# Where the lower halves of split matmul operands lie in on-chip memory

## The chip, the cores and the metric

The kernel runs on one core of one Trainium2 chip. The metric is the device time of one execution in microseconds (us), from three runs; beside them stands one profiled execution, from which all rows below come. In the profile PE is the matmul engine (TensorE) and PEld its weight loads, DVE is VectorE, ACT is ScalarE, POOL is GpSimd and SP is SyncE, which issues the transfers.

## The reference

One block of a diffusion transformer over 256 latent tokens and 256 context tokens, width 2048, all in float32. Cut to what matters here:

```
h  = modulate(rms_norm(x, norm_attn_w), sh_a, sc_a)        # also for ctx
q, k, v, u = split_projection(h @ w_in)                    # 2048 -> 2560
attn = latent_window_attention(q, k, v, kc, vc, attn_sink)
pool = multiscale_pool(u, pool_w, pool_scale)
x  = x + g_a * (concatenate([attn, pool]) @ w_out)         # 2048 -> 2048
hm = modulate(rms_norm(x, norm_mlp_w), sh_m, sc_m)
x  = x + g_m * (square(relu(hm @ w_up)) @ w_down)          # 2048 -> 8192 -> 2048
return rms_norm(x, final_norm_w)
```

The modulation vectors (sh, sc, g) come from `silu(c) @ w_ada + b_ada`.

## The kernel before

Every large product is made from split operands. An fp32 tile is cast to a shorter format (the upper part, `hi`, by ACT), and what is left over is its lower part (`lo = raw - hi`, by DVE). A product A*B then takes three matmuls into one accumulator, A_hi*B_hi, A_hi*B_lo and A_lo*B_hi, which the helper `mm3` issues at L288, L289 and L290. Each matmul instruction is preceded by a weight load of its stationary operand (128 columns); the other operand, 256 or 512 columns, moves through.

The weights stream from HBM in 1 MB tiles `raw` (five buffers), and are split in halves into `hi` and `lo` (six buffers each, `WeightStream.split_to`, L87 to L103). The stages, in the order of time, with the name of the accumulator that the profile shows:

- input projection: `ps_qu` (256 columns, weights stationary, activations `hhi`/`hlo` moving), `ps_k` (512 columns, the same way), `ps_v` (256 columns, weights moving);
- attention: scores `ps_s` (512 columns, keys `khi`/`klo` moving, queries `qs` stationary), transposes and `ps_o`;
- output projection: `ps_w` (512 columns, weights moving, the mixed activations `mx` stationary);
- the MLP. The first three of 16 column groups of w_up go through `mm3` at 256 columns. For the 13 others (`up_group`, L894) the upper and lower part of an activation tile `mx` lie side by side and move as one operand of 512 columns against `hi`, and then the upper part alone, 256 columns, against `lo`: for each quarter of the depth 16 matmuls of the first kind, then 16 of the second. `down_group` multiplies the activations `ahi`/`alo` (stationary) with w_down (`hi`/`lo` moving, 512 columns) through `mm3` into `ps_d`: eight groups b, each of 4 column blocks x 2 row halves x 8 depth tiles x 3 = 192 matmuls, 1536 in all, in which L288, L289 and L290 follow each other.

While one matmul runs, the weight load of the next one is already under way. The order on each engine is decided when the program is built. Tiles come from pools that are laid out in the order in which their tags are first asked for; `gap(pool, n)` asks for an unused tile of n bytes per partition, so that whatever follows lies n bytes further on. It computes nothing.

Of the kernel before, what the change touches and what calls it, by code (L numbers as in the profile page):

```python
# [9 lines left out]
F32R = mybir.dt.float32r  # L10
# [5 lines left out]
P = 128  # L16
D = 2048
KC = 16
T = 256
# [30 lines left out]
def gap(pool, n, name="gap"):  # L50

    pool.tile([P, n // 4], F32, tag=name, name=name, bufs=1)


class WeightStream:
# [27 lines left out]
    def split_to(self, n):  # L87
        nc = self.nc
        while self.n_half < min(n, len(self.halves)):
            i, h = self.halves[self.n_half]  # L90
            if i >= self.n_load:
                break
            raw = self.raw[i][:, 2 * h : 2 * h + 2, :]
            hi = self.pool.tile([P, 2, 512], F32R, tag="hi", name="hi", bufs=N_HALF)
            if not self.n_half:
                gap(self.pool, 320)
            lo = self.pool.tile([P, 2, 512], F32R, tag="lo", name="lo", bufs=N_HALF)
            nc.scalar.copy(hi, raw)  # L98
            nc.vector.tensor_tensor(lo, raw, hi.bitcast(F32), ALU.subtract)  # L99
            self.split[i, h] = (hi, lo)  # L100
            self.n_half += 1
# [23 lines left out]
def kernel(  # L125
# [223 lines left out]
    hpa = hpa_es.enter_context(tc.tile_pool(name="hpa", bufs=1, side="right", reuse_waits="tile"))  # L349
# [48 lines left out]
    def normalize(i):  # L398

        ss4 = stp.tile([P, 4], F32, tag="ss4", name="ss4", bufs=2)  # L400
        ss = stp.tile([P, 1], F32, tag="ss", name="ss", bufs=2)
        for q in range(4):
            junk = stp.tile([P, 512], F32, tag="junk", name="junk", bufs=2)
            xq = xh[i][:, 512 * q : 512 * q + 512]
            if q % 2:
                nc.scalar.activation(junk, xq, AF.Square, accum_out=ss4[:, q : q + 1])
            else:
                nc.vector.scalar_tensor_tensor(junk, xq, 1.0, xq, ALU.mult, ALU.mult, accum_out=ss4[:, q : q + 1])
        nc.vector.tensor_reduce(ss, ss4, axis=AX.X, op=ALU.add)
        r = rstd(stp, ss, 1)  # L410
        nc.vector.tensor_scalar(xh[i], xh[i], r, None, ALU.mult)
        for g in range(4):
            tp = bank("tp")
            for j in range(4):
                k = 4 * g + j
                nc.tensor.transpose(tp[:, P * j : P * j + P], xh[i][:, P * k : P * k + P], ident)
            nc.scalar.copy(xT[g][:, :, P * i : P * i + P], tp.rearrange("p (j t) -> p j t", j=4))
# [22 lines left out]
    def modulated(c_, streams=(0, 1)):  # L440

        pool = hpb if c_ in (2, 3, 6, 7) else hpa
        if 0 in streams:
            hhi = pool.tile([P, 2, 512], F32R, tag="hhi", name="hhi", bufs=2)
            if c_ in (0, 2):
                gap(pool, 320, "gaph")
            hlo = pool.tile([P, 2, 512], F32R, tag="hlo", name="hlo", bufs=2)
            hparts[c_] = hhi, hlo
        hhi, hlo = hparts[c_]
        for j in range(2):  # L450
            k = 2 * c_ + j
            xk = xT[k // 4][:, k % 4, :]
            for s in streams:
                v = xk[:, T * s : T * s + T]
                nc.vector.tensor_scalar(v, v, am_a[:, k, s : s + 1], sm_a[:, k, s : s + 1], ALU.mult, ALU.add)
            ts_ = slice(T * streams[0], T * streams[-1] + T)
            nc.scalar.copy(hhi[:, j, ts_], xk[:, ts_])  # L457
            nc.vector.tensor_tensor(hlo[:, j, ts_], xk[:, ts_], hhi[:, j, ts_].bitcast(F32), ALU.subtract)  # L458
            hs[k] = lambda s, j=j: (hhi[:, j, s], hlo[:, j, s])
# [72 lines left out]
    def run_in(op):  # L532
        if op[0] == "ada":
            c_, kg = op[1:]
            if kg == 0:
                adas[c_] = ada_attn(c_)
            adas[c_][kg]()
        elif op[0] == "mod":
            adas[op[1]][4]()
            modulated(op[1])  # L540
        elif op[0] == "kv":
            project_kv(*op[1:])
        elif op[0] == "qu":
            project_qu(*op[1:])
        elif op[0] == "mean":
            pool_mean(op[1])
        elif op[0] == "mixb":
            open_mixb()
        elif op[0] == "pool":
            in_w["pool"] = S.next("w")  # L550
        elif op[0] == "poolp":
            pool_project(op[1])
        elif op[0] == "pools":
            pool_split(op[1])
        else:
            run_late(1)

    mixa = hpb = None
    modulated(0, (0,))
    for op in in_ops:  # L560
        if op[0] == "ctx":
            normalize(2)
            normalize(3)
            modulated(0, (1,))
            xn_es.close()
            mixa = ctx.enter_context(tc.tile_pool(name="mixa", bufs=1, side="left", reuse_waits="tile"))
            gap(mixa, 192)
            hpb = hpb_es.enter_context(tc.tile_pool(name="hpb", bufs=1, side="left", reuse_waits="tile"))
            gap(hpb, 192)
        else:  # L570
            run_in(op)
    gap(hpa, 320)
    st_es.close()
    hpa_es.close()

# [222 lines left out]
    mp = ctx.enter_context(tc.tile_pool(name="mp", bufs=1, side="right", reuse_waits="tile"))  # L798
# [63 lines left out]

    def activation(pss):
        ahi = mp.tile([P, 4, T], F32R, tag="ahi", name="ahi", bufs=3)
        gap(mp, 64)
        alo = mp.tile([P, 4, T], F32R, tag="alo", name="alo", bufs=3)
        for m in range(4):
            t = mp.tile([P, T], F32, tag="act", name="act", bufs=2)
            if pss[m].shape[1] == T:
                nc.scalar.activation(t, pss[m], AF.Relu)  # L870
                nc.vector.tensor_tensor(t, t, t, ALU.mult)
            else:
                nc.scalar.copy(t, pss[m][:, T : 2 * T])
                nc.vector.tensor_tensor(t, pss[m][:, 0:T], t, ALU.add)
                nc.vector.scalar_tensor_tensor(t, t, 0.0, t, ALU.max, ALU.mult)
            nc.scalar.copy(ahi[:, m, :], t)
            nc.vector.tensor_tensor(alo[:, m, :], t, ahi[:, m, :].bitcast(F32), ALU.subtract)
        return ahi, alo

    def up_group():  # L880

        pss = [bank("ps_up") for _ in range(4)]
        for kg in range(4):
            w = S.next("w")
            for part in range(2):
                for m in range(4):
                    for j in range(4):  # L890
                        k = 4 * kg + j
                        wk = w(j, slice(P * m, P * m + P))[part]
                        ps, h = (pss[m][:, 0:T], hm[k][0]) if part else (pss[m], hm[k][2])
                        nc.tensor.matmul(ps, wk, h, start=part == k == 0, stop=part == 1 and k == KC - 1, skip_group_check=True)  # L894
        return activation(pss)

    def first_up_groups():

        banks = [bank("ps_up") for _ in range(6)]
        sums = [[banks[2 * f + m // 2][:, T * (m % 2) : T * (m % 2) + T] for m in range(4)] for f in range(3)]
        acts = []
        modulate_m(0)
        for kg in range(4):
            for f in range(3):
                w = S.next("w")
                if kg == f == 0:
                    with tc.issue_after(rb_ready.ins):  # L910
                        run_late(LATE_NORM)
                for m in range(4):
                    for j in range(4):
                        k = 4 * kg + j
                        mm3(sums[f][m], w(j, slice(P * m, P * m + P)), hm[k], k == 0 and m % 2 == 0, k == KC - 1)
                with tc.issue_after(rb_ready.ins):
                    run_late(LATE_UP[3 * kg + f])
                    if kg == 2 and f == 1:
                        run_late(1)
                if kg < 3 and f == 1:  # L920
                    modulate_m(kg + 1)
                if kg == 3:
                    acts.append(activation(sums[f]))
        return acts
# [133 lines left out]
```

## Time and profile before

| | us |
|---|---|
| three runs | 1160.4, 1165.46, 1166.04 |
| median of the three | 1165.46 |
| profiled execution, its own time | 1161.86 |
| span of the profiled execution | 1160.1 |
| PE busy | 1115.3 (96%) |
| DVE busy | 803.4 (69%) |
| ACT busy | 503.6 (43%) |

A matmul's time on the page (394 ns for 512 columns, say) goes from its start to its modelled end, and the next one starts long before that end. What a stream of matmuls costs is the distance from start to start, which the timeline gives; the page's mean cannot be multiplied by the count. A longer duration at the same number of columns does, however, go with a later start of the next matmul.

### The profile page before, as it was taken

The page shows a single profiled execution, that of the slowest core. Times are in us where ns is not written, and L with a number is a line of the kernel's source. Part 1 is how long each engine was busy: PE and PEld are TensorE (multiplying, and loading weights), DVE is VectorE, ACT ScalarE, POOL GpSimd, SP SyncE. Part 2 cuts the span into 40 slices and gives each one's busy share as a digit, 9 for nine tenths or more (in the row PEclk, how much of TensorE's full clock was granted, in tenths as well). Part 3 has the DMA queues.
Part 4 walks back from the last instruction along what each step waited for, and adds up shares of the span by engine and source line. Part 5 has one row for each costly group of instructions (what it writes and reads, how often), then busy time and mean ns, then how long its engine had stood idle before and what let it go on. Part 6 is the DMA issues. An engine that isn't in the chain of part 4 may idle for free.

```text
span 1160.1 us, 16052 instructions
## 1 busy us (share of the span) xinstructions
PE 1115.3 (96%) x6308; PEld 904.8 (78%) x6308; DVE 803.4 (69%) x1298; ACT 503.6 (43%) x760; POOL 40.4 (3%) x55
## 2 busy tenths in 40 slices
PE   3999999989999989999999999999999999999995
PEld 2767778845678869988888888888888888888884
DVE  5545567989786988886764884785664664587576
ACT  4532333357734433365443433443444443443452
POOL 1000001620000000000000000000000000000001
PEclk9899999989999989899999999999999999999998
DMA  9999897667898999968775775676566555655531
GB/s 337 317 328 340 298 311 258 218 232 271 278 378 276 312 316 358 353 225 267 267 268 190 252 257 188 235 251 231 182 189 199 192 181 184 199 191 189 183 107 73
DMA packets 174012, 286.64 MB, mean 247 GB/s; under 512 B 5609, under 2 KB 72353, under 8 KB 172785
## 3 DMA queue, kind: packets, MB, share of 16 engines
q1 hardware_dynamic: 172800, 279.55, 71.8%
q0 software_dynamic: 848, 5.55, 1.2%
q8 instruction: 49, 0.80, 0.3%
q10 hardware_dynamic: 288, 0.52, 0.1%
q14 instruction: 27, 0.21, 0.0%
HBM read 283.50 MB, written 2.10 MB: 246 GB/s over the span
## 4 chain that ended last, share of the span: by engine, by line
PE 81%; DVE 9%; DMA 6%; ACT 2%; issue 1%; SPq 1%; DVEq 0%; ACTq 0%
PE ps_up L894 25%; PE ps_d L288 10%; PE ps_d L289 10%; PE ps_d L290 10%; PE ps_ada L305 5%; DMA raw<-in_w_mlp_up_dram 3%; DVE lo L99 3%; PE ps_qu L288 2%; PE ps_qu L289 2%; PE ps_qu L290 2%; PE ps_o L738 2%; DMA raw<-in_w_in_dram 2%; DVE ada_v L327 1%; PE tp_p L727 1%; PE ps_w L288 1%
## 5 line engine op out<-in xcount | busy, mean ns | idle before, releaser
L99 DVE TENSOR_TENSOR lo<-raw,hi 128x1024 fp32r<-128x1024 f32 x330 | 396.8, 1224 | 223.1 <-ACT hi L98 216.1
L98 ACT CAST hi<-raw 128x1024 fp32r<-128x1024 f32 x330 | 337.5, 1051 | 407.3 <-PE ps_up L894 150.3
L288 PE MATMUL ps_d<-hi,ahi 128*128 128x512 f32 x512 | 201.6, 395 | 0.0
L289 PE MATMUL ps_d<-lo,ahi 128*128 128x512 f32 x512 | 201.0, 394 | 0.0
L894 PE MATMUL ps_up<-mx,hi 128*128 128x512 f32 x832 | 200.0, 392 | 0.0
L290 PE MATMUL ps_d<-hi,alo 128*128 128x512 f32 x512 | 198.4, 392 | 0.0
L894 PEld LDWEIGHTS ps_up<-mx,hi 128*128 128x128 f32 x832 | 153.4, 188 | 31.8 <-issue 1.9
L290 PEld LDWEIGHTS ps_d<-hi,alo 128*128 128x128 f32 x512 | 96.2, 188 | 22.8
L327 DVE SCALAR_TENSOR_TENSOR ada_v<-raw,c_sil,ada_v 128x512 f32<-128x512 f32 x135 | 100.8, 747 | 18.3 <-DMA raw<-in_w_ada_dram 16.8
L288 PEld LDWEIGHTS ps_d<-hi,ahi 128*128 128x128 f32 x512 | 96.2, 188 | 22.0
L289 PEld LDWEIGHTS ps_d<-lo,ahi 128*128 128x128 f32 x512 | 96.1, 188 | 21.2
L894 PEld LDWEIGHTS ps_up<-mx,lo 128*128 128x128 f32 x832 | 105.3, 189 | 4.0
L894 PE MATMUL ps_up<-mx,lo 128*128 128x256 f32 x832 | 106.6, 281 | 0.0
L288 PE MATMUL ps_qu<-hhi,hi 128*128 128x256 f32 x256 | 75.7, 296 | 5.4 <-ACT hhi L457 5.4
L305 PE MATMUL ps_ada<-raw,c_sil 128*32 128x512 f32 x480 | 73.1, 626 | 0.7 <-DMA raw<-in_w_ada_dram 0.7
L289 PE MATMUL ps_qu<-hlo,hi 128*128 128x256 f32 x256 | 72.9, 285 | 0.3 <-DVE hlo L458 0.3
L290 PE MATMUL ps_qu<-hhi,lo 128*128 128x256 f32 x256 | 72.7, 285 | 0.0
L288 PEld LDWEIGHTS ps_qu<-hhi,hi 128*128 128x128 f32 x256 | 49.2, 192 | 23.1 <-issue 10.9
L288 PE MATMUL ps_up<-mx,hi 128*128 128x256 f32 x192 | 54.4, 292 | 1.5 <-ACT mx L859 1.5
L289 PE MATMUL ps_up<-mx,hi 128*128 128x256 f32 x192 | 54.1, 286 | 0.0
L290 PE MATMUL ps_up<-mx,lo 128*128 128x256 f32 x192 | 53.0, 287 | 0.1
L290 PEld LDWEIGHTS ps_qu<-hhi,lo 128*128 128x128 f32 x256 | 48.9, 192 | 3.4 <-issue 1.7
(194 smaller groups left out, 1329.6 us busy)
## 6 DMA issues: line engine op xcount, KB each, us to landing
raw<-in_w_ada_dram SPq DMA_DIRECT2D x128, 512.0 KB, 7.2
raw<-in_w_mlp_up_dram SPq DMA_DIRECT2D x64, 1024.0 KB, 5.4
raw<-in_w_mlp_down_dram SPq DMA_DIRECT2D x64, 1024.0 KB, 5.1
raw<-in_w_ada_dram SPq DMA_DIRECT2D x32, 1024.0 KB, 6.4
raw<-in_w_in_dram SPq DMA_DIRECT2D x19, 1024.0 KB, 7.8
raw<-in_w_out_dram SPq DMA_DIRECT2D x16, 1024.0 KB, 7.4
xnat<-in_x_dram SPq DMA_DIRECT2D x2, 1024.0 KB, 6.2
xnat<-in_ctx_dram SPq DMA_DIRECT2D x2, 1024.0 KB, 11.6
```

Of the source, the lines that this page charges most:

```text
L98: nc.scalar.copy(hi, raw)
L99: nc.vector.tensor_tensor(lo, raw, hi.bitcast(F32), ALU.subtract)
L288: nc.tensor.matmul(ps, a[0], b[0], start=first, stop=False, skip_group_check=True)
L289: nc.tensor.matmul(ps, a[0], b[1], start=False, stop=False, skip_group_check=True)
L290: nc.tensor.matmul(ps, a[1], b[0], start=False, stop=last, skip_group_check=True)
L305: nc.tensor.matmul(ps[32 * j : 32 * j + 32, :], c_sil[:, 4 * kg + j, :], raw[:, j, :], start=(kg == 0), stop=(kg == 3), tile_position=(0, ...
L327: nc.vector.scalar_tensor_tensor(box["e"], raw[:, j, :], sc, box["e"], ALU.mult, ALU.add)
L727: nc.tensor.transpose(tp[:, P * k : P * k + P], self.p[:, i, P * k : P * k + P], ident)
L738: nc.tensor.matmul(ps[64 * i : 64 * i + 64, 0:T], va[k // 2][:, k % 2, 64 * g : 64 * g + 64], pT[:, k, i, :], start=(k == 0), stop=(k == 3 ...
L894: nc.tensor.matmul(ps, wk, h, start=part == k == 0, stop=part == 1 and k == KC - 1, skip_group_check=True)
```

## The change

No instruction is added, removed or moved: built, the two programs have the same instructions in the same order on all five engines, with the same waits, but for one: the transfer that loads the gate bias `ga` (GpSimd's queue, once) waits for earlier counts of PE and ACT. What differs is the address at which tiles lie. In bytes from the start of a partition, modulo 512, the operands of the split products lie at:

| tiles | before | after |
|---|---|---|
| `hi` / `lo` (weights) | 160 / 480 | 160 / 160 |
| `hhi` / `hlo` (input projection) | 352 / 160 | 352 / 352 |
| `mx` upper / lower (output projection, up) | 160 / 160 | 160 / 160 |
| `ahi` / `alo` (down) | 416 / 480 | 416 / 416 |
| `khi`, `klo`, `qs` (scores) | 288 | 288 |

Written as (moving, stationary), the three products of a stage, in the order L288, L289, L290, then see:

| stage | before | after |
|---|---|---|
| `ps_d` | (160, 416) (480, 416) (160, 480) | (160, 416) three times |
| `ps_w` | (160, 160) (480, 160) (160, 160) | (160, 160) three times |
| `ps_qu`, `ps_k` | (352, 160) (160, 160) (352, 480) | (352, 160) three times |
| `ps_v` | (160, 352) (480, 352) (160, 160) | (160, 352) three times |
| first three up groups | (160, 160) (160, 160) (160, 480) | (160, 160) three times |
| L894, 512 columns, then 256 | (160, 160), then (160, 480) | (160, 160) for both |

The diff:

```diff
@@ WeightStream.split_to
             hi = self.pool.tile([P, 2, 512], F32R, tag="hi", name="hi", bufs=N_HALF)
-            if not self.n_half:
-                gap(self.pool, 320)
             lo = self.pool.tile([P, 2, 512], F32R, tag="lo", name="lo", bufs=N_HALF)
@@ modulated
         if 0 in streams:
-            hhi = pool.tile([P, 2, 512], F32R, tag="hhi", name="hhi", bufs=2)
-            if c_ in (0, 2):
-                gap(pool, 320, "gaph")
-            hlo = pool.tile([P, 2, 512], F32R, tag="hlo", name="hlo", bufs=2)
+            hhi = pool.tile([P, 2, 512], F32R, tag=f"hhi{c_ % 2}", name="hhi", bufs=1)
+            hlo = pool.tile([P, 2, 512], F32R, tag=f"hlo{c_ % 2}", name="hlo", bufs=1)
             hparts[c_] = hhi, hlo
@@ the loop over the input projection
             mixa = ctx.enter_context(tc.tile_pool(name="mixa", bufs=1, side="left", reuse_waits="tile"))
-            gap(mixa, 192)
             hpb = hpb_es.enter_context(tc.tile_pool(name="hpb", bufs=1, side="left", reuse_waits="tile"))
             gap(hpb, 192)
         else:
             run_in(op)
-    gap(hpa, 320)
+    gap(hpa, 128)
@@ activation
         ahi = mp.tile([P, 4, T], F32R, tag="ahi", name="ahi", bufs=3)
+        alo = mp.tile([P, 4, T], F32R, tag="alo", name="alo", bufs=3)
         gap(mp, 64)
-        alo = mp.tile([P, 4, T], F32R, tag="alo", name="alo", bufs=3)
```

## Rows read from the trace of the kernel before

**Rows 1.** The page: the span, and PE's busy time, share and instructions.

```profile
span 1160.1 us, 16052 instructions
PE 1115.3 (96%) x6308; PEld 904.8 (78%) x6308; DVE 803.4 (69%) x1298; ACT 503.6 (43%) x760; POOL 40.4 (3%) x55
```

**Rows 2.** Four stretches: length, busy time per engine, PE clock, DMA share, GB/s.

```profile
60.00:250.00 190.00, 184.33 (x1325) 139.93 (x1324) 129.35 (x228) 66.02 (x102) 31.91 (x37) 0.98 0.85 286
...
315.00:505.00 190.00, 183.48 (x1108) 158.44 (x1107) 156.75 (x237) 78.19 (x111) 1.31 (x2) 0.96 0.94 322
505.00:1160.00 655.00, 643.26 (x3193) 541.43 (x3192) 431.71 (x576) 278.86 (x370) 4.08 (x3) 0.99 0.62 205
```

**Rows 3.** Who waited for whom, 505 to 1160 us: total us, times, longest.

```profile
ACT hi L98 <- PE ps_up L894: 150.3, 51, 3.5
ACT hi L98 <- PE ps_d L290: 130.3, 92, 3.5
...
PEld ps_up L894 <- issue: 1.9, 8, 0.2
```

**Rows 4.** The chain that ended last, 505 to 1160 us, by line.

```profile
by line: PE ps_up L894 44.0%; PE ps_d L288 17.7%; PE ps_d L289 17.6%; PE ps_d L290 17.5%; PE ps_gm L943 0.5%; DVE rs_v L274 0.3%; DVE y L986 0.2%; DVE t L982 0.2%; DVE t L981 0.2%; DVE rs_u L282 0.2%; DVE rs_y L283 0.2%; DVE rs_u L281 0.1%;
```

**Rows 5.** By source line: duration in ns, min/median/max; first and last start in us.

```profile
L288 PE MATMUL ps_d<-hi,ahi x512: 387/395/401, 501.4 to 1147.4; 128*128 128x512 f32 x171
L289 PE MATMUL ps_d<-lo,ahi x512: 387/394/398, 501.6 to 1147.6; 128*128 128x512 f32 x171
L290 PE MATMUL ps_d<-hi,alo x512: 387/391/402, 501.8 to 1147.9; 128*128 128x512 f32 x171
L894 PE MATMUL ps_up<-mx,hi x832: 387/389/792, 546.3 to 1101.6; 128*128 128x512 f32 x167
L894 PE MATMUL ps_up<-mx,lo x832: 280/281/283, 550.4 to 1103.6; 128*128 128x256 f32 x167
```

**Rows 6.** Timeline of PE in one down group, its first and last rows: start us, us.

```profile
658.52 0.40 PE L288 MATMUL ps_d<-hi,ahi 128*128 128x512 f32 x1
...
700.11 0.40 PE L288 MATMUL ps_d<-hi,ahi 128*128 128x512 f32 x1
...
700.81 0.40 PE L288 MATMUL ps_d<-hi,ahi 128*128 128x512 f32 x1
...
702.89 1.02 PE L943 MATMUL ps_gm<-ada_v,ones 128*128 128x512 f32 x2
```

**Rows 7.** Timeline of PE in an up group, read from two starts (709.30 and 710.46).

```profile
709.30 3.81 PE L894 MATMUL ps_up<-mx,hi 128*128 128x512 f32 x16
710.46 2.65 PE L894 MATMUL ps_up<-mx,hi 128*128 128x512 f32 x11
712.96 0.52 PE L894 MATMUL ps_up<-mx,lo 128*128 128x256 f32 x3
```

**Rows 8.** Timeline of PE in the output projection: five triples, then the next operation.

```profile
354.62 0.40 PE L288 MATMUL ps_w<-hi,mx 128*128 128x512 f32 x1
...
358.10 0.28 PE L335 MATMUL ps_adac<-ones,ada_v 128*128 128x2 f32 x2
```

**Rows 9.** By source line, input projection at 256 columns: ns, min/median/max.

```profile
L288 PE MATMUL ps_qu<-hhi,hi x256: 277/283/583, 30.5 to 229.6; 128*128 128x256 f32 x128
L289 PE MATMUL ps_qu<-hlo,hi x256: 276/281/582, 31.4 to 229.8; 128*128 128x256 f32 x128
L290 PE MATMUL ps_qu<-hhi,lo x256: 277/282/415, 31.8 to 229.9; 128*128 128x256 f32 x128
```

## The prediction

> **What bounds the kernel now.** I read the page first: PE is busy 96% of a span of 1160.1 us [rows 1], an average that a stretch table has to split. From 60 to 250 us PE is busy 184 of 190 us, but DMA share is 0.85 and DVE has 129 us of work; from 315 to 505 us (output projection, first up groups) DMA share is 0.94 at 322 GB/s; from 505 to 1160 us (the rest of the MLP) DMA share is 0.62, DVE works 432 and ACT 279 of 655 us [rows 2]. So one looks for PE as the only bound in the last stretch, and the waits confirm it: there ACT, which makes `hi` and so frees and fills weight buffers, waits 150.3 us for PE at L894 and 130.3 us for PE at L290, while PE's weight loads wait 1.9 us in all [rows 3]. The chain that ended last is in this stretch 44.0% L894 and 17.7 + 17.6 + 17.5% `ps_d` [rows 4]. A nanosecond per matmul taken from `ps_d` or L894 shortens the span at full value; in the other stretches only in part.
>
> The next view is the duration of one matmul, by line, since no instruction changes and only such durations can. All these matmuls are alike in shape (512 columns, 128 rows), and yet the median is 389 ns at L894, where every operand pair is (160, 160), and 395, 394 and 391 ns in `ps_d`, whose products alternate between three pairs [rows 5]. The timeline turns this into distances. In a down group, first start 658.52 and next operation 702.89 us: 192 matmuls in 44.37 us, 231.1 ns each; inside, one triple takes 700.81 - 700.11 = 0.70 us, 232 each [rows 6]. In an up group the first five starts of a run take 710.46 - 709.30 = 1.16 us, 232 ns each, and the eleven after them 712.96 - 710.46 = 2.50 us, 227 each [rows 7]. The 5 ns between 232 and 227 are the 5 or 6 ns between 394 and 389: the same stall, seen twice. So a stream with one pair of places runs some matmuls at 232 and then settles at 227; a stream whose places alternate never does.
>
> **The change, part by part.** It adds and removes no instruction, so there is nothing to cost but durations.
>
> *Down, `ps_d`.* After the change all three products see (160, 416). If they settle at 389 ns as L894 does, each triple gains (395 - 389) + (394 - 389) + (391 - 389) = 13 ns [rows 5], and 1536 / 3 = 512 triples gain 6.7 us. By distances: (231.1 - 227) x 1536 = 6.3 us [rows 6, 7], with the rounding of the timeline (0.01 us in 2.50, so 1 ns per start) between 4.8 and 7.8. Each of the eight groups pays five unsettled starts at its beginning, 5 x 5 ns x 8 = 0.2 us. I take 6.5. The bounds: L894 has moving and stationary places equal, `ps_d` will have them 256 bytes apart, and no row shows a settled stream at that distance. If the distance matters, the median could lie anywhere from the 387 ns that is the shortest of all lines to the 401 of the longest `ps_d` at L288 [rows 5]; in the sum that is from (393.3 - 387) x 1536 = 9.7 us gained to (401 - 393.3) x 1536 = 11.8 us lost, 393.3 being the mean of the three medians. I take 389, the median of the only long stream with constant places.
>
> *Up, L894.* The 832 matmuls at 512 columns keep their places: 0. The 832 at 256 columns go from (160, 480) to (160, 160). The nearest rows are the three lines of `ps_qu`, 283, 281 and 282 ns at three different pairs, against 281 here [rows 5, 9]: at 256 columns places move a duration by 2 ns at most. So 0, with 2 x 832 = 1.7 us at most either way.
>
> *Output projection, `ps_w`.* 128 triples go to (160, 160), exactly L894's case. Now 15 matmuls take 358.10 - 354.62 = 3.48 us, 232 each [rows 8]; at 227 the stage's 384 matmuls take 1.9 us less. But the stretch has DMA share 0.94 [rows 2], so that a faster PE waits sooner for the next weights; between 0 and 1.9, I take 0.4, since most of the stretch is paced by transfers.
>
> *Input projection.* `ps_k` (96 matmuls at 512 columns, priced like `ps_w`: 5 ns) gives 0.5 us, `ps_qu` with 283, 281, 282 against 281 [rows 9] gives 256 x 3 ns = 0.8 us, in a stretch that shares its bound with DMA and DVE [rows 2]. Of 0 to 1.3 us I take 0.3.
>
> *DVE and ACT* write `lo` and `hi` at other addresses. They stay behind PE by the waits of [rows 3], 280 us in all; should each split take a little longer, that is the work that hides it, and without this cover DVE, at 432 of 655 us [rows 2], would still not be the bound. The transfer of `ga`, the one instruction whose wait changes, is used only in the output projection: 0.
>
> The sum: 6.5 + 0.4 + 0.3 = 7.2 us. On the profiled execution's own time, 1161.86 us, that gives 1154.7. The three runs lie from 1160.4 to 1166.04, their median 1165.46 is 3.6 us above the profiled one; I do not know which of them the next session will resemble, and put the median after the change halfway, at 1154.7 + 1.8 = 1156.5 us.
>
> **A rule that speaks against it.** The rows show the same instruction at 389 and at 395 ns, at a granted clock of 0.99 of the full 2.4 GHz in the stretch [rows 2, 5]. The Trainium skill, "TensorE: Matmul & The Clock Gate", section "Step-by-step: what each phase is for", says that PE has two independent read ports, one for the moving operand and one for weight loads, so that loading the next weights takes no bandwidth from the running matmul. By that rule the place of one operand against the other cannot matter, and the sum would be 0. The same page, section "Back-to-back issue gap", gives N/2.4 + 2.5 ns, 216 ns for 512 columns; no stream here comes to it, the best being 227. I weigh the rule as the second rival below.
>
> **The rivals.** *Slower: the pair (160, 416) settles high.* Constant places do not guarantee 227: the first five of L894's run go at 232 with the same pair [rows 7]. If the down stream settled at the 398 ns that L289 reaches at its longest [rows 5], the loss is (398 - 393.3) x 1536 = 7.2 us: 1161.86 + 7.2 + 1.8 = 1170.9 us. It decides from 397 ns on, where 1536 x 3.8 ns passes 5.8 us. For it speaks that `ps_d` alone will have a distance of 256 bytes that no settled stream has now. The rows on that distance are divided: while L288 runs and while L290 runs, the moving operand lies at 160 and the next weights come from 416, that very pair, and the one takes 395 ns, the other 391 [rows 5].
>
> *No change: places are not the cause.* Down differs from L894 in more than its places: weights move there and activations stand still. `ps_w`, with weights moving too and its stationary place constant, also runs at 232 [rows 8], which fits this rival as well as it fits the moving place that alternates there. Then all durations stay: 1161.86 + 1.8 = 1163.7 us. Against it: L894 itself shows both speeds with roles unchanged.
>
> *No change: the stream does not settle.* The down stream keeps the gait of the first five of L894, 232 against 231.1 now: 0.9 x 1536 = 1.4 us lost, less 0.7 from the other stages: about 1164.4 us.
>
> **How the numbers follow.** Chances: forecast 0.52, places without effect 0.12, not settling 0.15, settling high 0.21. A measurement of this kernel can tell about 0.5% from no change, 5.8 us. The forecast's 7.2 us is only a little beyond that; with runs that differ by 5.6 us I count four fifths of its chance as faster, the rest as same. So faster 0.42; same 0.10 + 0.26 = 0.36; slower 0.22, the high case with a little of the unsettled one. The forecast's own range is 1150.5 to 1159.7 (lowest run 1160.4 less the largest sum, 6.7 + 1.9 + 1.3; highest run 1166.0 less 6.3). For 8 in 10 the range must take in both cases without change and the edge of the slower one: 1151 to 1168.
>
> **What would show it.** Right: in the durations by line L288, L289 and L290 of `ps_d` all at 389 ns, a down group of 192 in 43.6 us in place of 44.4, `ps_w` at 389 as well, L894 at 389 and 281 as before, and the gain found between 505 and 1160 us. Wrong at the first step: `ps_d` stays at 391 to 395. Wrong at the distance of 256 bytes: `ps_w` drops to 389 and `ps_d` does not, or rises. Wrong at the bound: durations drop, but PE begins to wait for `lo` or `raw` in the last stretch. Wrong at 256 columns: L894's 281 or the 281 to 283 of the input projection move by more than 2 ns.

## The result, and the profile after

The changed kernel takes 1155.54 us (median of seven runs, 1153.37 to 1160.22) against 1162.25 us for the kernel before (seven runs, 1160.4 to 1166.04, the three of the section on the time before among them): a ratio of 0.9937, 95% interval 0.9917 to 0.9958. The profiled execution takes 1156.12 us, its span is 1154.4 us, 5.7 less than the 1160.1 of [rows 1].

The page of the changed kernel, its span and PE's line:

```profile
span 1154.4 us, 16052 instructions
PE 1107.1 (96%) x6308; PEld 904.9 (78%) x6308; DVE 804.4 (70%) x1298; ACT 503.8 (44%) x760; POOL 39.5 (3%) x55
```

The same count of instructions, the same work on DVE and ACT, and 8 us less of PE. Durations by source line of the changed kernel, min/median/max in ns (its L286 to L288 are the L288 to L290 of before, its L889 is L894):

```profile
L286 PE MATMUL ps_d<-hi,ahi x512: 389/389/396, 501.0 to 1141.6; 128*128 128x512 f32 x171
...
L287 PE MATMUL ps_d<-lo,ahi x512: 389/389/398, 501.2 to 1141.8; 128*128 128x512 f32 x171
...
L288 PE MATMUL ps_d<-hi,alo x512: 388/389/396, 501.4 to 1142.0; 128*128 128x512 f32 x171
...
L889 PE MATMUL ps_up<-mx,hi x832: 387/389/799, 545.0 to 1096.6; 128*128 128x512 f32 x167
...
L889 PE MATMUL ps_up<-mx,lo x832: 277/283/283, 549.1 to 1098.6; 128*128 128x256 f32 x167
```

Against [rows 5], the three lines of `ps_d` went from 395, 394 and 391 to 389 each; L894 kept its 389 at 512 columns, and at 256 columns went from 281 up to 283. The timeline of PE gives the distances (start us, us): two up groups, 256 matmuls, from 611.68 to 656.64, then a down group of 192 to 700.19.

```profile
611.68 0.80 PE L889 MATMUL ps_up<-mx,hi 128*128 128x512 f32 x1
...
656.64 0.40 PE L286 MATMUL ps_d<-hi,ahi 128*128 128x512 f32 x1
...
700.19 1.02 PE L938 MATMUL ps_gm<-ada_v,ones 128*128 128x512 f32 x2
```

A down group takes 43.55 us, 226.8 ns from start to start, against 44.37 and 231.1 in [rows 6]: 0.82 x 8 = 6.6 us. Two up groups take 44.96 us. In the kernel before they started, by the same view, here, and ended with the 658.52 of [rows 6]:

```profile
613.78 0.79 PE L894 MATMUL ps_up<-mx,hi 128*128 128x512 f32 x1
```

That is 44.74, so 0.22 us per two groups or 1.4 us over the 13 groups were lost again. The first down matmul starts at 501.0 where it started at 501.4, which is all that the stages ahead of it left. On the way there more was won and lost again. The output projection, before and after, and then the first rows of PE behind it, before and after:

```profile
L288 PE MATMUL ps_w<-hi,mx x128: 387/395/793, 315.2 to 411.0; 128*128 128x512 f32 x128
...
L286 PE MATMUL ps_w<-hi,mx x128: 387/389/799, 313.4 to 407.6; 128*128 128x512 f32 x128
```

```profile
412.25 0.63 PE L809 MATMUL tp_x<-ident,x 128*128 128x128 f32 x4 [0.35 <-DVE x L829]
...
410.46 0.63 PE L804 MATMUL tp_x<-ident,x 128*128 128x128 f32 x4 [2.05 <-DVE x L824]
```

The changed kernel begins the output projection 1.8 us earlier and its last triple 3.4 us earlier, but then PE waits 2.05 in place of 0.35 us for `x` from DVE. Down, up and these stages together: 6.6 - 1.4 + 0.4 = 5.6 of the 5.7 us between the spans.

The bound is where it was. Waits of the changed kernel from 505 to 1154 us (total us, times, longest): ACT still waits for PE, and PE's weight loads wait for 1.9 us in all.

```profile
ACT hi L96 <- PE ps_up L889: 151.4, 51, 3.6
ACT hi L96 <- PE ps_d L288: 125.6, 93, 3.4
...
PEld ps_up L889 <- issue: 1.9, 8, 0.2
```

### The profile page after: what moved, and what is told of

Its sections match the earlier page's. It is cut to its first block, busy times and chain, and to the rows that moved or that the text cites. A ratio compares the mean times of both kernels' runs of the same rounds, so it can differ in the third digit from the quotient of the medians.

```text
span 1154.4 us, 16052 instructions
## 1 busy us (share of the span) xinstructions
PE 1107.1 (96%) x6308; PEld 904.9 (78%) x6308; DVE 804.4 (70%) x1298; ACT 503.8 (44%) x760; POOL 39.5 (3%) x55
## 4 chain that ended last, share of the span: by engine, by line
PE 83%; DVE 8%; DMA 5%; ACT 2%; issue 1%; SPq 1%; DVEq 0%; ACTq 0%
PE ps_up L889 25%; PE ps_d L288 10%; PE ps_d L286 10%; PE ps_d L287 10%; PE ps_ada L303 5%; PE ps_qu L286 2%; PE ps_qu L288 2%; PE ps_qu L287 2%; DVE lo L97 2%; PE ps_o L733 2%; DMA raw<-in_w_in_dram 2%; DMA raw<-in_w_mlp_up_dram 1%; PE ps_up L286 1%; DVE ada_v L325 1%; PE ps_up L287 1%
## 5 line engine op out<-in xcount | busy, mean ns | idle before, releaser
L889 PE MATMUL ps_up<-mx,hi 128*128 128x512 f32 x832 | 200.1, 393 | 0.0
L286 PE MATMUL ps_d<-hi,ahi 128*128 128x512 f32 x512 | 198.8, 389 | 0.0
L287 PE MATMUL ps_d<-lo,ahi 128*128 128x512 f32 x512 | 198.6, 389 | 0.0
L288 PE MATMUL ps_d<-hi,alo 128*128 128x512 f32 x512 | 196.9, 389 | 0.0
L889 PEld LDWEIGHTS ps_up<-mx,hi 128*128 128x128 f32 x832 | 153.4, 188 | 31.7 <-issue 1.9
L288 PEld LDWEIGHTS ps_d<-hi,alo 128*128 128x128 f32 x512 | 96.1, 188 | 20.0
L286 PEld LDWEIGHTS ps_d<-hi,ahi 128*128 128x128 f32 x512 | 96.1, 188 | 19.7
L889 PEld LDWEIGHTS ps_up<-mx,lo 128*128 128x128 f32 x832 | 106.7, 191 | 4.0
L889 PE MATMUL ps_up<-mx,lo 128*128 128x256 f32 x832 | 107.9, 283 | 0.0
L286 PE MATMUL ps_qu<-hhi,hi 128*128 128x256 f32 x256 | 75.0, 293 | 5.4 <-ACT hhi L453 5.4
L288 PE MATMUL ps_qu<-hhi,lo 128*128 128x256 f32 x256 | 72.2, 283 | 0.0
L286 PEld LDWEIGHTS ps_qu<-hhi,hi 128*128 128x128 f32 x256 | 48.9, 191 | 23.1 <-issue 10.1
L286 PE MATMUL ps_up<-mx,hi 128*128 128x256 f32 x192 | 54.8, 294 | 1.5 <-ACT mx L854 1.5
L288 PE MATMUL ps_up<-mx,lo 128*128 128x256 f32 x192 | 53.1, 287 | 0.0
L288 PEld LDWEIGHTS ps_qu<-hhi,lo 128*128 128x128 f32 x256 | 48.9, 192 | 3.4 <-DVE lo L97 1.7
```

What stands on the lines that cost most here:

```text
L286: nc.tensor.matmul(ps, a[0], b[0], start=first, stop=False, skip_group_check=True)
L287: nc.tensor.matmul(ps, a[0], b[1], start=False, stop=False, skip_group_check=True)
L288: nc.tensor.matmul(ps, a[1], b[0], start=False, stop=last, skip_group_check=True)
```

## The experiments

Places below are bytes modulo 512, as in the table of the change; the distance of a pair is moving less stationary, modulo 256 (why 256, the second experiment shows). Each run but the last three is one execution with its profile; its medians repeat over hundreds of instructions, and it is read by these and not by its total time.

**One operand alternates, the other stands.** The forecast rested on constant places, and left open which operand has to be constant. The first run takes the changed kernel and puts `lo` back to 480 (the gap in `mixa` keeps all other tiles at their places):

```diff
+            if not self.n_half:
+                gap(self.pool, 320)
             lo = self.pool.tile([P, 2, 512], F32R, tag="lo", name="lo", bufs=N_HALF)
...
+            gap(mixa, 192)
```

> The changed kernel with lo of the weights put back at 480 and alo left at 416: in ps_d the moving place alternates (160, 480, 160), the stationary place is constant. Theory M (a stream settles when its moving operand keeps its place): ps_d stays at medians of 391 to 395 ns, a down group of 192 matmuls takes 44.4 us or more. Theory S (the stationary place is what has to be constant): ps_d settles at 389 ns, 43.6 us a group. Theory P (the whole pair has to be constant): 391 to 395 as well. The up groups see (160, 160) and (160, 480) as before the change and take 281 ns at 256 columns under all three.

The second moves `alo` alone:

```diff
+        gap(mp, 64)
         alo = mp.tile([P, 4, T], F32R, tag="alo", name="alo", bufs=3)
-        gap(mp, 64)
```

> The changed kernel with alo moved to 480: in ps_d the moving place is constant at 160, the stationary place alternates (416, 416, 480). Theory M: ps_d settles at 389 ns, 43.6 us a group, as if nothing had been undone. Theory S and theory P: 391 to 395 ns, 44 us or more. Everything outside ps_d as in the changed kernel under all.

Durations by source line (min/median/max, ns), moving place alternating:

```profile
L288 PE MATMUL ps_d<-hi,ahi x512: 387/395/402, 502.1 to 1149.3; 128*128 128x512 f32 x171
...
L289 PE MATMUL ps_d<-lo,ahi x512: 387/395/398, 502.3 to 1149.5; 128*128 128x512 f32 x171
...
L290 PE MATMUL ps_d<-hi,alo x512: 387/393/402, 502.6 to 1149.8; 128*128 128x512 f32 x171
...
L892 PE MATMUL ps_up<-mx,lo x832: 280/281/283, 551.2 to 1105.3; 128*128 128x256 f32 x167
```

The same, stationary place alternating:

```profile
L286 PE MATMUL ps_d<-hi,ahi x512: 387/389/398, 501.1 to 1148.3; 128*128 128x512 f32 x171
...
L287 PE MATMUL ps_d<-lo,ahi x512: 387/392/398, 501.3 to 1148.6; 128*128 128x512 f32 x171
...
L288 PE MATMUL ps_d<-hi,alo x512: 389/397/400, 501.5 to 1148.8; 128*128 128x512 f32 x171
```

A down group of the first run, by the timeline:

```profile
659.39 0.40 PE L288 MATMUL ps_d<-hi,ahi 128*128 128x512 f32 x1
...
703.95 0.59 PE L941 MATMUL ps_gm<-ada_v,ones 128*128 128x512 f32 x1
```

Either alternation alone brings the whole stall back: three medians of 395, 395 and 393 sum to 16 ns over 3 x 389, and 389, 392 and 397 to 11, against 13 before the change; a down group takes 44.56 us in the first run and, from 658.36 to 702.73, 44.37 in the second, the 44.37 of before. So theory M (only the moving place counts) and theory S (only the stationary place) both fall, and P stands: the pair has to be constant. The last line of the first run shows as well that the 281 ns of the up groups return with the pair (160, 480).

**How far apart is the same place?** Two runs set `lo` 256 and 128 bytes from `hi`, with the gap of the first experiment at 256 and 128 (and `mixa`'s at 256 and 384).

> The changed kernel with lo at 416, 256 bytes from hi (160): moving place in ps_d and ps_w alternates by 256 bytes. If places count modulo 512: unsettled, 391 ns or more, 44.4 us a group. If they count modulo 256 or a smaller power of two: settled, 389 ns and 43.6 us. L894 (its line in the kernel before) at 256 columns sees (160, 416): between 281 and 283 ns, no theory says which.

> The changed kernel with lo at 288, 128 bytes from hi: moving place alternates by 128 bytes. If places count modulo 128: settled, 389 ns and 43.6 us a down group, and the 256-column matmuls of the up groups at 283 ns as with lo at 160. If modulo 256 or 512: unsettled, 391 ns or more, 44.4 us.

Durations with 256 bytes:

```profile
L288 PE MATMUL ps_d<-hi,ahi x512: 389/389/396, 502.3 to 1142.9; 128*128 128x512 f32 x171
...
L289 PE MATMUL ps_d<-lo,ahi x512: 389/389/398, 502.5 to 1143.2; 128*128 128x512 f32 x171
...
L892 PE MATMUL ps_up<-mx,lo x832: 277/283/284, 550.4 to 1099.9; 128*128 128x256 f32 x167
```

And with 128:

```profile
L288 PE MATMUL ps_qu<-hhi,hi x256: 276/276/582, 30.8 to 226.2; 128*128 128x256 f32 x128
...
L289 PE MATMUL ps_d<-lo,ahi x512: 387/394/395, 499.9 to 1147.2; 128*128 128x512 f32 x171
...
L892 PE MATMUL ps_up<-mx,lo x832: 278/284/288, 548.3 to 1103.1; 128*128 128x256 f32 x167
```

256 bytes count as the same place, in `ps_d` and at 256 columns (283 as at distance 0); 128 bytes do not. The 512 in the words of the change is twice what the chip counts. One row looks like a surprise: `ps_qu`, whose stationary place here alternates by 128 bytes, runs at 276 ns, where its median in the changed kernel is 281. But the median hides two levels there. Two stretches of `ps_qu` in the changed kernel, with one pair of places, (352, 160), in both:

```profile
L286 PE MATMUL ps_qu<-hhi,hi x6: 281/281/281, 88.0 to 89.8; 128*128 128x256 f32 x6
...
L286 PE MATMUL ps_qu<-hhi,hi x6: 276/276/277, 120.4 to 122.1; 128*128 128x256 f32 x6
```

At 256 columns a constant pair can settle at 276 or at 281 ns. The four runs above, one profiled execution each, took 1163.74 us (moving place alternates), 1162.77 (stationary), 1157.44 (256 bytes) and 1161.35 (128), the kernel before beside them 1161.74.

**Does any constant pair settle?** The changed `ps_d` sees (160, 416), which modulo 256 is distance 0, the same as L894. `ps_k`, constant too but at distance 192, still has 394 to 396 ns after the change. Theory C says that any constant pair settles at 389 ns, theory D that the distance decides the level. Three runs move the activations to other distances: `mx` (up and output projection) to 352, and then, together, `mx` and `ahi`/`alo` to 288 and to 224. The first of them, with the others' gaps in words (`mixa` 128 and 64, `hpb` 64 and 128, and 192 and 256 in place of 64 after `alo`):

```diff
             mixa = ctx.enter_context(tc.tile_pool(name="mixa", bufs=1, side="left", reuse_waits="tile"))
+            gap(mixa, 192)
...
-            gap(hpb, 192)
```

> The changed kernel with the activations mx at 352 in place of 160: all products of the up groups and of the output projection still see one pair, moving and stationary 192 bytes apart (modulo 256) in place of 0. Theory C (any constant pair settles): L894's line at 512 columns stays at 389 ns, ps_w too, and the 256-column matmuls return from 283 to the 281 that they had at that distance before the change: about 1.4 us faster than the changed kernel. Theory D (the distance decides at which level a stream settles; ps_k has distance 192 in the changed kernel and walks between 231 and 236 ns from start to start): 512 columns at 394 ns and 233.5 from start to start, 832 x 5 ns = 4 to 6 us slower than the changed kernel. ps_d as in the changed kernel under both.

> The changed kernel with mx at 288 (up and output projection: distance 128, moving less stationary, modulo 256) and ahi and alo at 288 (down: distance 128 as well). Theory C: 389 ns at 512 columns in all three stages. Theory D: another level, the same in up and down, between 226.7 and 233.5 ns from start to start. For the 256-column matmuls, which run at 117.7 at distance 192 and at 119.6 at distance 0, no theory says.

> The changed kernel with mx at 224 (up and output projection: distance 64) and ahi and alo at 224 (down: distance 192 modulo 256). Theory C: 389 ns at 512 columns everywhere. Theory D: the down stream at 233.5 from start to start as ps_k, so 192 x 233.5 = 44.8 us a down group; up at a level of its own.

A fourth sets `mx` and `ahi`/`alo` to 192, and `hhi`/`hlo` to 160 (gaps of 32 in `mixa`, 480 in `hpb`, 320 in `hpa`, 288 after `alo`):

> The changed kernel with mx at 192 (up and output projection: distance 32), ahi and alo at 192 (down: distance 224) and hhi and hlo at 160 (input projection: distance 0). Theory C: 389 ns at 512 columns everywhere, ps_k included. Theory D: ps_k, now at distance 0, settles at 389 ns and 227 from start to start as ps_d did, in place of 394 and 233.5; ps_qu, now at distance 0, goes from 281 to the 283 ns of the up groups; up and down at levels of their own.

Durations, the run with `mx` at 352:

```profile
L889 PE MATMUL ps_up<-mx,hi x832: 388/394/793, 545.4 to 1096.3; 128*128 128x512 f32 x167
...
L889 PE MATMUL ps_up<-mx,lo x832: 276/276/283, 549.5 to 1098.2; 128*128 128x256 f32 x167
```

The run with 288, its durations, then the timeline of a down group:

```profile
L286 PE MATMUL ps_d<-hi,ahi x512: 390/393/404, 500.0 to 1152.1; 128*128 128x512 f32 x171
...
L890 PE MATMUL ps_up<-mx,hi x832: 387/393/794, 545.1 to 1106.0; 128*128 128x512 f32 x167
```

```profile
928.96 0.39 PE L286 MATMUL ps_d<-hi,ahi 128*128 128x512 f32 x1
...
973.58 0.40 PE L890 MATMUL ps_up<-mx,hi 128*128 128x512 f32 x1
```

The run with 224, the same two views:

```profile
L286 PE MATMUL ps_d<-hi,ahi x512: 393/394/398, 499.6 to 1148.0; 128*128 128x512 f32 x171
...
L890 PE MATMUL ps_up<-mx,hi x832: 387/392/798, 544.9 to 1101.8; 128*128 128x512 f32 x167
...
L890 PE MATMUL ps_up<-mx,lo x832: 276/279/283, 549.0 to 1103.8; 128*128 128x256 f32 x167
```

```profile
925.85 0.40 PE L286 MATMUL ps_d<-hi,ahi 128*128 128x512 f32 x1
...
970.65 0.40 PE L890 MATMUL ps_up<-mx,hi 128*128 128x512 f32 x1
```

The run with 192:

```profile
L286 PE MATMUL ps_d<-hi,ahi x512: 393/396/399, 503.2 to 1155.5; 128*128 128x512 f32 x171
...
L286 PE MATMUL ps_k<-hhi,hi x32: 388/395/501, 55.7 to 190.4; 128*128 128x512 f32 x32
...
L287 PE MATMUL ps_k<-hlo,hi x32: 387/392/504, 56.0 to 190.6; 128*128 128x512 f32 x32
...
L288 PE MATMUL ps_k<-hhi,lo x32: 388/389/397, 56.3 to 190.8; 128*128 128x512 f32 x32
...
L890 PE MATMUL ps_up<-mx,hi x832: 390/395/798, 548.4 to 1109.3; 128*128 128x512 f32 x167
L890 PE MATMUL ps_up<-mx,lo x832: 277/280/283, 552.6 to 1111.3; 128*128 128x256 f32 x167
```

Theory C falls in every run, and D stands. At 512 columns the medians by distance are 389 (0), 395 (32, up), 392 (64, up), 393 (128, up and down alike), 394 (192; up, down and `ps_k` alike) and 396 (224, down). From start to start, a down group of 192 takes 43.55 us at distance 0 (226.8 ns), 973.58 - 928.96 = 44.62 at 128 (232.4) and 970.65 - 925.85 = 44.80 at 192 (233.3); at 224 it is again 44.80 (932.23 to 977.03). The median of up at 64 misleads: its matmuls repeat 388, 392 and 394 ns, and a run of 16 takes 3.68 us (724.96 to 728.64), against 3.65 at distance 0 and 3.73 at 32, 128 and 192. The roles do not matter: down has its weights moving and up has them standing, and equal distances give equal medians. The output projection agrees. Its weights move, so that it has distance 64 in the run with 352 (not 192, as expected) and 128, 192 and 224 in the others: 388 to 394, then 393, 394, and 395 to 396 ns.

Where matmuls come in short runs, distance 0 is little help. `ps_k`, moved to distance 0, drops from 394, 394 and 396 to 395, 392 and 389 ns, so that only the third product reaches the 389 that theory D expected. In its longest run, 24 matmuls from 185.59 us, every one from the sixth on takes 389 ns; most of its runs are shorter than 12, and the slow starts at their head [rows 7] set the median. The scores have had distance 0 all along (288 for all three tiles) and keep medians of 397 and 393 in the changed kernel: they come four at a time. `ps_qu` at distance 0 goes from 281 to 283 ns, as expected.

With the levels known, a further rival falls: that every matmul runs at the level of its own distance, and alternation merely mixes levels. With the moving place alternating the three distances are 0, 64 and 0, an estimated mean of 228 ns (226.8 twice, and 3.68 us / 16 = 230), and 44.56 us / 192 = 232 were measured; with the stationary place alternating they are 0, 0 and 192, a mean of 229, and 231 were measured. What no run tried is another place for the upper weight parts: `hi` lies at 160 in every one of these streams.

One profiled execution each, these runs took 1155.73 us (352), 1166.52 (288), 1162.50 (224) and 1170.01 (192). The first is worth a look: 512 columns lost 394 - 389 there, as D says, but at 256 columns L894 runs at 276 ns, and the two nearly cancel (two up groups take 44.85 us, 612.04 to 656.89, against 44.96).

**A version beyond the change.** Distance 0 is best at 512 columns and one of the slowest at 256 (283 ns; only the 284 of 128 bytes, above, is slower). Two kernels therefore keep the change, but put the lower weight parts of the 13 late up groups, which only the 256-column matmuls read, 64 or 224 bytes further on. The buffers of `lo` grow by 256 bytes each, and the output projection's `t` has two buffers in place of three to make room:

```diff
-            lo = self.pool.tile([P, 2, 512], F32R, tag="lo", name="lo", bufs=N_HALF)
+            lo = self.pool.tile([P, 1088], F32R, tag="lo", name="lo", bufs=N_HALF)
+            at = 56 if i in self.shifted else 0
+            lo = lo[:, at : at + 1024].rearrange("p (j c) -> p j c", j=2)
...
     def add_up(f, kg):
+        if f >= 3:
+            S.shifted.add(len(S.items))
...
-            t = wop.tile([P, 512], F32, tag="t", name="t", bufs=3)
+            t = wop.tile([P, 512], F32, tag="t", name="t", bufs=2)
```

(16 in place of 56 for 64 bytes. With the larger buffers, neighbouring buffers of `lo` differ by 256 bytes modulo 512, which by the second experiment counts as nothing.) With them the changed kernel ran again.

> The changed kernel once more, as the measure for the two beside it: about 0.994 of the kernel before, 43.55 us a down group, 44.5 to 45.0 us for two up groups (256 matmuls).

> The changed kernel, but the lower weight parts of the 13 late up groups lie 64 bytes further on inside larger buffers (so that two buffers of t in the output projection replace three, to make room): down and 512 columns of up keep distance 0, the 256-column matmuls of up have distance 192 modulo 256. Theory D with one level per distance, read from the kernel before, where this very pair of streams stands: 281 ns and 117.8 from start to start in place of 119.6, so two up groups in 44.3 to 44.7 us, 1.4 us less in all than the changed kernel, ratio about 0.9925. If the level of the run with mx at 352 holds instead (276 ns, 113.5): 5 us less, ratio about 0.9895. If distance has nothing to do with it: no difference from the changed kernel. The down groups at 43.55 us under all.

> The same with the lower weight parts 224 bytes further on: the 256-column matmuls of up at distance 32. Theory D, from the run with mx at 192: 280 ns, 116.8 from start to start, 832 x 2.8 ns = 2.3 us less than the changed kernel, ratio about 0.992. If a stream keeps the level at which it comes out of the 512-column run before it, another level that no run shows. The down groups at 43.55 us.

| kernel | median us | ratio to the kernel before, 95% |
|---|---|---|
| changed, again | 1155.8 | 0.9939 (0.9919 to 0.9959) |
| `lo` of up 64 bytes on | 1155.2 | 0.9931 (0.9915 to 0.9947) |
| `lo` of up 224 bytes on | 1152.3 | 0.9906 (0.9888 to 0.9925) |

Durations with 64 bytes, then with 224:

```profile
L894 PE MATMUL ps_up<-mx,lo x832: 280/281/283, 549.6 to 1097.8; 128*128 128x256 f32 x167
```

```profile
L894 PE MATMUL ps_up<-mx,hi x832: 387/389/799, 544.0 to 1093.5; 128*128 128x512 f32 x167
L894 PE MATMUL ps_up<-mx,lo x832: 277/279/282, 548.1 to 1095.5; 128*128 128x256 f32 x167
```

The timeline of the latter, two up groups and the down group behind them:

```profile
610.52 0.80 PE L894 MATMUL ps_up<-mx,hi 128*128 128x512 f32 x1
...
655.15 0.40 PE L291 MATMUL ps_d<-hi,ahi 128*128 128x512 f32 x1
...
698.71 0.59 PE L943 MATMUL ps_gm<-ada_v,ones 128*128 128x512 f32 x1
```

44.63 us for two up groups in place of 44.96, 0.33 x 6.5 = 2.1 us over 13; the down group keeps 43.56. With 64 bytes 281 ns return, as expected, and not the 276 of the run with `mx` at 352, though the distance is 192 in both: `ps_qu` showed the same two levels at this distance. Two up groups take 44.74 us there (612.17 to 656.91), 1.4 us less over 13. The intervals of the three overlap, but all four runs with 224 bytes (1149.71 to 1153.04) lie below all runs of the other two (from 1153.14). The timeline accounts for 2.1 of the 3.5 us between the medians of 224 bytes and of the changed kernel. Another 1.1 us of the profiled executions lie ahead of the first down matmul, at 499.97 in place of 501.09; with 64 bytes it starts at 501.56, though up to there these two kernels have the same places. So this part is no gain of the places, and against 64 bytes the timeline gives 224 only 0.11 x 6.5 = 0.7 us.

## Why the prediction was right

*The bound* was read right: the whole of the 6.6 us taken from `ps_d` reached the end, and PE did not begin to wait in the last stretch.

*Down* was forecast at 6.5 us and measured at 6.6, by the step that carried it: all three medians at 389. But the reason given, one pair of places, was only half of it. The second half is the distance: (160, 416) is 256 bytes apart, which counts as 0. The bound set for "if the distance matters" was the right doubt. With places only 128 bytes further apart, equally constant, a down group takes 44.62 us, 0.25 more than before the change, and the same forecast would have been wrong. The rival that settles high thus describes something real, at another distance than the one that the change happened to have. That it had distance 0 in `ps_d` was, for the prediction, luck: its text counts the 256 bytes as a distance. (Its triple of 0.70 us is 233 ns each and not 232; no term rests on it.)

*Up at 256 columns* was taken as 0, with 1.7 us at most either way, since three pairs of `ps_qu` lay within 2 ns. It lost 1.4 us, inside that bound; the mistake was to take its middle. The three pairs of `ps_qu` alternated, so that their medians could not tell what a constant pair takes. L894 went from (160, 480) to distance 0, one of the slowest at this length.

*The stages ahead* were put at 0.7 us (0.4 and 0.3), and the start of the down groups came 0.4 us earlier. The sum was near by luck, for its parts were not. The output projection began 1.8 us earlier, more than the 1.3 us that the input projection could give at most by the forecast: part of `ps_qu` settled at 276 ns, where the forecast took 281 for all of it. `ps_w` at 389 won 3.4 - 1.8 = 1.6 us, nearly the 1.9 that the forecast took as a limit. Of these 3.4 us 3.0 were lost again, but not to waits for weights as forecast: 1.7 in the wait of PE for `x` from DVE, and the rest in the modulation product behind it and in the first three up groups, whose 256 columns went from 281 and 282 to 283 ns. Pricing `ps_k` like `ps_w` failed: at distance 192 it kept 394 to 396 ns and gave nothing.

*The rival that places are no cause* fell with the result, since nothing but addresses changed. The same instruction takes 389 to 396 ns by the distance of the two operands' places (medians), and a constant moving place with an alternating stationary one is enough to bring the stall back. By the Trainium skill, "TensorE: Matmul & The Clock Gate", section "Step-by-step: what each phase is for", PE has two independent read ports, and loading the next weights takes no read bandwidth from the running matmul. The prediction drew from this, as a rival, that the place of one operand against the other could not matter; in this kernel it does. Where the two operands meet, no run here shows.

*The total*, 1156.5 forecast and 1155.54 measured, is better than its parts, and in that luck too: the sum of 7.2 us was 5.7 in the spans and 6.7 in the medians, and the forecast started from 1161.86 + 1.8 = 1163.7 us, where the median of before turned out as 1162.25 with more runs.

## What to carry to other kernels

Where PE is the bound and every matmul loads new weights, look at the median duration by source line at equal shapes: differences of a few ns (389 against 395) are worth as much as the distance from start to start says, here 2% of a stage. Then compare the addresses of the moving and the stationary operand, and try to keep the pair constant along a stream and, at 512 columns, at the same place modulo 256 bytes; at 256 columns try several distances. A change that makes places equal is not good by itself: the constant distances of 128, 192 and 224 bytes (44.62, 44.80 and 44.80 us a down group) were slower than the mixture before (44.37). And look at single runs beside the median by line: in `ps_qu` one median stood for two levels.

## What the runs showed of the hardware

- At 512 columns the matmul stream takes from 226.8 ns (distance 0) to 233.3 (distances 192 and 224) from start to start, by the places of its operands alone; 256 bytes count as no distance, 128 do.
- Alternation of the moving place by 320 bytes or of the stationary one by 64 keeps the medians between 389 and 397 ns, at a mean of 232 and 231 from start to start, above the mean of the levels of the distances that take turns (228 and 229).
- At 256 columns medians from 276 to 284 ns occur, and one pair of places has more than one level: (352, 160) runs at 276 and at 281 ns within the changed kernel, in `ps_qu`, long before the first 512 columns of up. What decides between the two is open.
